# The token scale of two output norms: a block turn, two DRAM round trips and GpSimd in place of ones products, root and reciprocal

## The chip, the cores and the metric

The kernel runs on one core of a Trainium2 chip, as one launch. The metric is the device time of one execution in microseconds (us). The engines named below are TensorE (PE, matrix products), VectorE (DVE), ScalarE (ACT), GpSimd (POOL) and SyncE (SP, which only issues transfers). Each engine works through its own instruction list in order; an instruction whose inputs are not there holds everything behind it on that engine. TensorE's list and, in parts of the program, those of the other engines are in the order in which the program was written; elsewhere a scheduler sets the order when the program is built.

## What is computed

One layer of a bidirectional encoder: a combined input projection, eight attention heads, a gated linear recurrence in both directions, an RMS norm of each of the two groups, gates, and an output projection. The lines that bear on this change:

```python
def rms_norm(x, w):
    y = x * lax.rsqrt(jnp.mean(x * x, axis=-1, keepdims=True) + EPS)
    return y * w

mixed = jnp.concatenate([rms_norm(attn_out, attn_norm_w) * jax.nn.silu(g_attn),
                         rms_norm(lru_out, lru_norm_w) * jax.nn.silu(g_lru)], axis=-1)
return x + jnp.einsum('bse,ed->bsd', mixed, w_out)
```

There are 512 tokens; each group is 1024 wide. In the kernel both groups lie with features on the 128 partitions and tokens along the row, so a token's mean of squares is a sum over partitions (and over eight feature tiles), and its 1/rms is wanted on every partition.

## The kernel before, in words

Almost all the time is products in three parts (each float32 factor is split into a high and a low half, `mm3`, lines 153 to 155). Weights come as raw tiles `wr` of 128x2x512 through SP (`wraw`, line 206) into a ring of three; ACT casts the high half `wh` (line 218), DVE subtracts for the low half `wl` (line 219), and TensorE multiplies. A raw slot is free again once DVE has subtracted from it.

The stages in order: the recurrence's input projections, k and v, q in two halves (`both`), then the gate projections (`gates`) into which the attention is woven, the last gate projection (`later` woven in), and the output products (line 1029).

The group scales are made twice. For the recurrence group, `kv` runs beside the q projections: `lru_squares` sums squares into `hsum` (DVE line 568, POOL line 570), and then `halved` (lines 821 and 822) splits that sum, `spread` lets TensorE multiply both halves by a matrix of ones (line 829), which leaves the token's sum on all partitions, ACT takes the root (line 830) and DVE the reciprocal in four pieces (line 834). The result is `gbc`, 128x512. `normed` (line 839) multiplies the recurrence outputs `hs` by it on DVE. For the attention group the same happens in `later`, with `asum` (POOL line 751) in, and `normed` on the attention outputs `av`.

Two other things stand beside this. Sums of quarters of the output weights are built in DRAM by transfers that add (`add_to`, line 905): POOL issues them, 128x512 each, and SP copies what they add to. And at the very start, `busy` (line 1156) lets TensorE multiply ones while the first data are on the way: 11 such fillers (`WARM`) and then 3 (`WARM2`) between the first four turning products (line 253) and the first real products (line 388).

The order around the change: TensorE's is written out by hand. SP's, POOL's, ACT's and DVE's are the scheduler's near the first place (about 205 to 260 us), and SP's is by hand in the attention and POOL's, ACT's and DVE's by the scheduler near the second (about 420 to 460 us).

Of the kernel before, what the change touches and what calls it, by code (L numbers as in the profile page):

```python
# [11 lines left out]
F32 = mybir.dt.float32  # L12
F32R = mybir.dt.float32r
AF = mybir.ActivationFunctionType
ALU = mybir.AluOpType
AX = mybir.AxisListType

P = 128
SEQ = 512
DM = 2048  # L20
KT = DM // P
NT = SEQ // P
HD = 128
NH = 8
NKV = 2
G = NH // NKV
NB = 8
EPS = 1e-6
# [11 lines left out]
SOON = 150  # L40


WARM, WARM2 = 11, 3


BEGIN, STEPS, LATE = 11, 2, 3
# [5 lines left out]
B = 32  # L52
TURNED = 5
NQ = P // B
# [9 lines left out]
def hybrid_kernel(  # L64
# [20 lines left out]
    nc = tc.nc  # L85
# [4 lines left out]
    pools, order = {}, {"left": [], "right": []}  # L90

    def opened(name, side):
        pools[name] = tc.alloc_tile_pool(name=name, bufs=1, side=side, reuse_waits="tile")
        order[side].append(name)
        return pools[name]
# [18 lines left out]
    dram = ctx.enter_context(tc.tile_pool(name="dram", bufs=1, space=bass.MemoryType.DRAM))  # L114
# [3 lines left out]
    def nm(s):  # L118
        cnt[0] += 1
        return f"{s}_{cnt[0]}"  # L120
# [22 lines left out]
    def mm():  # L143
        return ps.tile([P, SEQ], F32, tag="mm", name=nm("mm"))

    def const(shape, name, dt=F32):
        return cp.tile(list(shape), dt, tag=name, name=name)

    def f(ap):
        return ap.bitcast(F32)  # L150
# [11 lines left out]
    ones_r = const([P, P], "ones_r", F32R)  # L162
    nc.gpsimd.memset(f(ones_r), 1.0)
    nhalf = const([P, 48], "nhalf")
# [44 lines left out]
    turn_of, split_done = [0], {}  # L209
# [33 lines left out]
    def behind(those):  # L243
        stack = ExitStack()
        for ins in those:
            stack.enter_context(tc.issue_after(ins))
        return stack
# [44 lines left out]
    def bring_back(to, aside_):  # L292

        src = aside_.rearrange("(i c) b x -> b c i x", c=B)
        for b in range(NQ):
            nc.sync.dma_start(
                to[b * B : (b + 1) * B].rearrange("p i k t r -> p i (k t r)"), src[b]
            )

    def in_order(v):  # L300
        return v.rearrange("p (t i r) -> p i t r", t=NT, i=NQ)
# [40 lines left out]
    last_pool = [None]  # L342
# [86 lines left out]
    def drain(fill):  # L429
        for _ in fill:  # L430
            pass
# [30 lines left out]
    sums = {}  # L462
# [97 lines left out]
    def lru_squares():  # L560

        hsum = pools["rot"].tile([P, 2, SEQ], F32, tag="hsum", name="hsum")
        nc.scalar.activation(hsum, hp[0], AF.Square)
        for pair in hp[1:]:
            yield 2
            sq = pools["rot"].tile([P, 2, SEQ], F32, tag="hsq", bufs=1, name=nm("hsq"))
            nc.scalar.activation(sq, pair, AF.Square)
            nc.vector.tensor_add(hsum, hsum, sq)
        sums["l"] = hsum[:, 0, :]
        nc.gpsimd.tensor_add(sums["l"], sums["l"], hsum[:, 1, :])  # L570
# [29 lines left out]
    def norm_rope(es, nh, tab):  # L600

        es = [e[:, : nh * HD].rearrange("p (h d) -> p h d", d=HD) for e in es]
        rs = []
        for e in es:
            r = pools["rot"].tile([P, nh], F32, tag=f"rr{nh}", bufs=NT, name=nm("rr"))
            for h in range(nh):
                sq = pools["rot"].tile([P, HD], F32, tag="sh", bufs=1, name=nm("sh"))
                nc.scalar.activation(sq, e[:, h, :], AF.Square, accum_out=r[:, h : h + 1])
            rsqrt_mean(r, r, HD, nh)
            rs.append(r)  # L610
        for t, (e, r) in enumerate(zip(es, rs)):
            sq = pools["rot"].tile([P, nh, HD], F32, tag="sq", bufs=2, name=nm("sq"))
            nc.vector.tensor_mul(e, e, r[:, :, None].broadcast_to([P, nh, HD]))
            for s in range(2):
                nc.vector.tensor_mul(
                    sq.rearrange("p h (a s d) -> p h a s d", s=2, d=32)[:, :, :, s, :],
                    e.rearrange("p h (a s d) -> p h a s d", s=2, d=32)[:, :, :, 1 - s, :],
                    tab[:, t, 1, :].rearrange("p (a s d) -> p a s d", s=2, d=32)[:, None, :, s, :]
                    .broadcast_to([P, nh, 2, 32]),
                )  # L620
            nc.vector.tensor_mul(e, e, tab[:, t, 0, :][:, None, :].broadcast_to([P, nh, HD]))
            nc.vector.tensor_add(e, e, sq)
        return es

    kth, ktl = [None] * NKV, [None] * NKV
# [5 lines left out]
    def sent(es, nh, *us):  # L631

        us = us or [
            pools["rot"].tile([P, NQ, 2, NT, B], F32, tag="uq", bufs=2, name=nm("uq"))
            for _ in range(nh // 2)
        ]
        for n, u in enumerate(us):
            for t, e in enumerate(es):
                blocks(u, t, e[:, 2 * n : 2 * n + 2].rearrange("p h d -> p (h d)"))
            yield  # L640
            asides.append(put_aside(u, "qd", 5))

    def landed(aside_):

        to = pools["qkv"].tile([P, NQ, 2, NT, B], F32, tag="lq", bufs=2, name=nm("lq"))
        bring_back(to, aside_)
        return to

    def split_head(pair, k, hi, lo):
        src = pair[:, :, k]  # L650
        hi, lo = (in_order(v) for v in (hi, lo))
        return nc.scalar.copy(hi, src).ins, nc.vector.tensor_sub(lo, src, f(hi)).ins

    def kv(es):
        turned_k = sent(norm_rope(es, NKV, rk), NKV)
        yield 20
        opened("wx", "right")
        for t in range(NT):
            vv = es[t][:, NKV * HD :]
            vt = pools["qkv"].tile([P, 2, NKV * HD], F32R, tag="v", bufs=NT, name=nm("v"))  # L660
            vh[t], vl[t] = vt[:, 0, :], vt[:, 1, :]
            nc.scalar.copy(vh[t], vv)
            nc.vector.tensor_sub(vl[t], vv, f(vh[t]))
        yield from lru_squares()
        yield 2
        drain(turned_k)
        yield 6
        pair = landed(asides.pop(0))
        for h in range(NKV):
            yield (12, 4)[h]  # L670
            kt = pools["qkv"].tile([P, 2, SEQ], F32R, tag="kt", bufs=NKV, name=nm("kt"))
            kth[h], ktl[h] = kt[:, 0, :], kt[:, 1, :]
            those = split_head(pair, h, kth[h], ktl[h])
        parts = halved(
            sums["l"],
            lambda: pools["rope"].tile([P, SEQ], F32R, tag="kv", bufs=NT, name=nm("kv")),
            those,
        )
        yield 4
        spread(gbc, parts, NB * P)  # L680

    qs = {}

# [127 lines left out]
    def fin_s(shape=(P, SEQ), dt=F32):  # L811
        return pools["fin"].tile(list(shape), dt, tag="s", bufs=2, name=nm("s"))

    eps = const([P, 48], "eps")
    nc.gpsimd.memset(eps, EPS)

    def halved(src, tile_of, those=()):

        hi, lo = tile_of(), tile_of()
        with behind(those):  # L820
            nc.scalar.copy(hi, src)
            nc.vector.tensor_sub(lo, src, f(hi))
        return hi, lo

    def spread(dst, parts, n, those=()):

        pb = mm()
        for k, part in enumerate(parts):
            nc.tensor.matmul(pb, ones_r, part, start=k == 0, stop=k == 1)  # L829
        nc.scalar.activation(dst, pb, AF.Sqrt, scale=1.0 / n, bias=eps[:, :1])  # L830
        for t in range(NT):
            ts_ = slice(t * P, (t + 1) * P)
            with behind(those):
                nc.vector.reciprocal(dst[:, ts_], dst[:, ts_])

    gbc = const([P, SEQ], "gbc")

    def normed(pair):
        nc.vector.tensor_mul(pair, pair, gbc[:, None, :].broadcast_to([P, 2, SEQ]))
# [372 lines left out]
    for step in proj_feat(C_XR, a1, first, given):  # L1212
# [8 lines left out]
        c, e = step  # L1221
# [123 lines left out]
    def build(i, pair, parts):  # L1345
        mixed[i][1] = parts
        seven(pair, *parts)
# [5 lines left out]

    def later():
        with tc.high_priority():
            parts = halved(sums["a"], lambda: fin_s(dt=F32R))
        yield 2
        with tc.high_priority():
            spread(gbc, parts, NH * HD, split_done[turn_of[0] - 2][1:])
        yield 4  # L1360
        for pair in ap_[:2]:
            normed(pair)
        yield 4
        todo = gate(late, ap_[:2], R_AN, fin_s)
        for _ in range(3):
            yield next(todo)
        build(4, ap_[0], [hring.tile([P, 7, H], F32R, name=nm(t)) for t in ("mh", "ml")])
        yield from todo
        for pair in ap_[2:]:
            normed(pair)  # L1370

    acc = []
    wsums = last_sums()
    fill = with_sums(proj_feat(C_GA + SEQ, acc, take=take), 1, 8, 8 + 2 * NP)
    weave(fill, later())
    drain(fill)
    closed("xw")
# [71 lines left out]
```

## Time and profile before

| | us |
|---|---|
| median of three runs (626.97, 627.20, 628.66) | 627.2 |
| the profiled execution | 626.85 |
| its span, first to last instruction | 625.1 |
| DVE busy | 494.5 |
| ACT busy | 352.5 |
| POOL busy | 101.7 |

The profile shows one execution. The span is the time between the first and the last instruction; the 1.75 us between span and execution lie outside it. In a row of the timeline the first number is the start, the second how long the row lasts (the first start to the last end, where several instructions are merged, with their count after an x), then engine, line, operation, what is written and read, and in brackets how long the engine sat idle before and what released it. A matrix product of 512 columns is recorded with some 0.39 us, but starts follow each other every 0.23 us, since they are pipelined.

### The profile page before, as it was taken

What the parts mean: (1) busy time and instruction counts of PE and PEld (TensorE: products, weight loads), DVE (VectorE), ACT (ScalarE), POOL (GpSimd) and SP (SyncE); (2) the same over time, 40 slices, a digit from 0 to 9 for tenths busy, and PEclk for the clock granted to TensorE, in tenths of its full rate; (3) what the DMA queues carried; (4) which work ended last, traced back from release to release, by engine and by line L of the source; (5) the groups of instructions that cost most, each with busy time, mean ns of one, the idle gap of its engine ahead of it and who ended that gap; (6) DMA issues with size and microseconds to landing.
All of it is one profiled execution on the core that took longest, in us unless ns stands there. A gap on an engine that the chain in (4) does not pass through costs nothing.

```text
span 625.1 us, 8277 instructions
## 1 busy us (share of the span) xinstructions
PE 619.9 (99%) x2756; PEld 512.5 (82%) x2756; DVE 494.5 (79%) x796; ACT 352.5 (56%) x617; POOL 101.7 (16%) x134
## 2 busy tenths in 40 slices
PE   9999999999999999999999999999999999999997
PEld 7888888888888888888888888888888888888886
DVE  5967979986699875987887888549978866886886
ACT  3764899379935823555475447428445633443441
POOL 0000211112003622622122222100310101010010
PEclk9999999999999999999999999999999999999999
DMA  8987775859774599489668646923995676896262
GB/s 289 303 227 224 182 198 171 179 134 198 233 232 139 169 245 242 104 204 271 187 179 254 201 143 192 265 76 107 270 243 183 209 253 228 297 339 226 70 202 101
DMA packets 73595, 127.61 MB, mean 204 GB/s; under 512 B 6617, under 2 KB 29265, under 8 KB 73553
## 3 DMA queue, kind: packets, MB, share of 16 engines
q1 hardware_dynamic: 65664, 109.65, 56.8%
q0 software_dynamic: 7712, 17.31, 14.3%
q8 instruction: 21, 0.34, 0.2%
q14 instruction: 22, 0.17, 0.1%
q10 hardware_dynamic: 176, 0.14, 0.1%
HBM read 110.29 MB, written 37.75 MB: 237 GB/s over the span
## 4 chain that ended last, share of the span: by engine, by line
PE 99%; ACT 0%; DVE 0%; issue 0%; POOL 0%; POOLq 0%
PE pj L153 20%; PE pj L155 20%; PE pj L154 20%; PE mm L1029 14%; PE pj L1029 11%; PE mm L155 3%; PE mm L153 3%; PE mm L154 3%; PE pj L388 2%; PE mm L253 1%; PE mm L1156 0%; PE mm L829 0%; ACT x L258 0%; PE mm L367 0%; DVE cb L1058 0%
## 5 line engine op out<-in xcount | busy, mean ns | idle before, releaser
L153 PE MATMUL pj<-x,wh 128*128 128x512 f32 x368 | 143.5, 390 | 0.0
L155 PE MATMUL pj<-x,wl 128*128 128x512 f32 x368 | 143.2, 389 | 0.0
L154 PE MATMUL pj<-x,wh 128*128 128x512 f32 x368 | 143.2, 389 | 0.0
L218 ACT CAST wh<-wr 128x512 fp32r<-128x512 f32 x142 | 84.5, 617 | 79.3 <-PE pj L154 31.7
L219 DVE TENSOR_TENSOR wl<-wr,wh 128x512 fp32r<-128x512 f32 x144 | 99.5, 720 | 19.6 <-ACT wh L218 18.5
L881 ACT CAST wh<-wr 128x1024 fp32r<-128x1024 f32 (+1 forms) x72 | 60.7, 861 | 75.0 <-PE mm L1029 37.5
L882 DVE TENSOR_TENSOR wl<-wr,wh 128x1024 fp32r<-128x1024 f32 (+1 forms) x72 | 68.7, 984 | 30.3 <-ACT wh L881 30.0
L155 PEld LDWEIGHTS pj<-x,wl 128*128 128x128 f32 x368 | 69.1, 188 | 14.5
L154 PEld LDWEIGHTS pj<-x,wh 128*128 128x128 f32 x368 | 69.1, 188 | 14.3
L153 PEld LDWEIGHTS pj<-x,wh 128*128 128x128 f32 x368 | 69.1, 188 | 14.2
L153 PE MATMUL pj<-wh,x 128*128 128x512 f32 x192 | 74.7, 389 | 0.0
L155 PE MATMUL pj<-wh,x 128*128 128x512 f32 x192 | 74.7, 389 | 0.0
L154 PE MATMUL pj<-wl,x 128*128 128x512 f32 x192 | 74.7, 389 | 0.0
L905 POOL DMA_DIRECT2D t<-in_w_out_dram x40 | 33.6, 906 | 157.7 <-DMA t<-in_w_out_dram 99.9
L1029 PE MATMUL mm<-wh,ml 128*128 128x512 f32 x126 | 49.0, 389 | 0.0
L1029 PE MATMUL mm<-wh,mh 128*128 128x512 f32 x126 | 49.0, 389 | 0.0
L1029 PE MATMUL mm<-wl,mh 128*128 128x512 f32 x126 | 49.0, 389 | 0.0
L154 PEld LDWEIGHTS pj<-wl,x 128*128 128x128 f32 x192 | 36.0, 188 | 7.6
L155 PEld LDWEIGHTS pj<-wh,x 128*128 128x128 f32 x192 | 36.0, 188 | 7.5
L153 PEld LDWEIGHTS pj<-wh,x 128*128 128x128 f32 x192 | 36.0, 188 | 7.4
L706 POOL TENSOR_SCALAR p<-p,sm 128x512 f32<-128x512 f32 x32 | 24.3, 762 | 89.3 <-DVE sm L705 89.3
L1029 PE MATMUL pj<-wl,mh 128*128 128x512 f32 (+1 forms) x100 | 38.5, 385 | 0.0
(201 smaller groups left out, 1050.8 us busy)
## 6 DMA issues: line engine op xcount, KB each, us to landing
wr<-in_w_in_dram SPq DMA_DIRECT2D x71, 512.0 KB, 5.0
wr<-in_w_out_dram SPq DMA_DIRECT2D x24, 512.0 KB, 5.2
t<-in_w_out_dram POOLq DMA_DIRECT2D x40, 256.0 KB, 7.3
wr<-t SPq DMA_DIRECT2D x40, 256.0 KB, 5.6
pd<-u SPq DMA_DIRECT2D x16, 512.0 KB, 3.0
pt<-pd SPq DMA_DIRECT2D x64, 128.0 KB, 3.9
t<-in_w_out_dram SPq DMA_DIRECT2D x24, 256.0 KB, 5.3
t<-t SPq DMA_DIRECT2D x16, 256.0 KB, 5.4
```

What stands on the lines that cost most here:

```text
L153: nc.tensor.matmul(acc, lh, rh, start=start, stop=False)
L154: nc.tensor.matmul(acc, lh, rl, start=False, stop=False)
L155: nc.tensor.matmul(acc, ll, rh, start=False, stop=stop)
L218: copy(hi, raw[:, k, :]).ins,
L219: nc.vector.tensor_sub(lo, raw[:, k, :], f(hi)).ins,
L253: nc.tensor.transpose(pt[:, t * P : (t + 1) * P], xc[:, t, ks], ident)
L388: nc.tensor.matmul(acc[e], w[:, e * P : (e + 1) * P], x_[2 * c + k], start=c == k == j == 0, stop=False,)
L706: last_pool[0] = nc.gpsimd.tensor_scalar(p, p, sm, 0.0, op0=ALU.mult, op1=ALU.add).ins
L881: nc.scalar.copy(hi[:, to], b)
L882: nc.vector.tensor_sub(lo[:, to], b, f(hi[:, to]))
L905: nc.gpsimd.dma_start(dst, src, accum_op=ALU.add)
L1029: nc.tensor.matmul(dst[s][:, es], lh[:, ts_], rh[:, es], start=i == ends_[0] and j == 0, stop=i == ends_[1] and j == 2,)
```

## The change

`halved` and `spread` are replaced by `token_scale`. It turns the 128x512 sums in blocks of 32x32 on DVE, so that in each quarter of the partitions a row is one token of a block, and sums each block's 32 columns (128x16). These four partial sums per token go to DRAM and come back side by side on 32 partitions (first round trip). GpSimd adds the four, scales, adds EPS and raises to the power -0.5 on a 32x16 tile. The 512 results go to DRAM as one row and come back to all 128 partitions (second round trip), and GpSimd copies them into `gbc` in token order. It is a generator: its parts are set between other steps by `next`. The fillers before the first products go from 3 to 5.

```diff
-WARM, WARM2 = 11, 3
+WARM, WARM2 = 11, 5
...
+        scale = token_scale(
+            gbc, sums["l"], NB * P,
+            lambda: pools["rope"].tile([P, SEQ], F32, tag="kv", bufs=NT, name=nm("kv")),
+        )
         for h in range(NKV):
-            yield (12, 4)[h]
+            for n in ((3, 3, 3, 3), (2, 2))[h]:
+                yield n
+                if (h, n) != (1, 2):
+                    next(scale)
...
-            those = split_head(pair, h, kth[h], ktl[h])
-        parts = halved(sums["l"], ..., those)
-        yield 4
-        spread(gbc, parts, NB * P)
+            split_head(pair, h, kth[h], ktl[h])
...
+    def token_scale(dst, src, n, tile_of):
+        turned, small = tile_of(), tile_of()
+        nj = SEQ // B
+        nc.vector.transpose(turned, src)
+        part = small[:, :nj]
+        nc.vector.reduce_sum(part, turned.rearrange("p (j c) -> p j c", c=B), axis=AX.X)
+        there = dram.tile([NQ, B, nj], F32, name=nm("parts"), tag="parts")
+        row = dram.tile([1, SEQ], F32, name=nm("row"), tag="row")
+        nc.sync.dma_start(there.rearrange("b r j -> (b r) j"), part)
+        yield
+        back = small[:B, 2 * B : 2 * B + NQ * nj].rearrange("r (b j) -> r b j", b=NQ)
+        nc.sync.dma_start(back, there.rearrange("b r j -> r b j"))
+        s = small[:B, 5 * B : 5 * B + nj]
+        with tc.issue_after(last_pool[0]):
+            nc.gpsimd.tensor_add(s, back[:, 0], back[:, 1])
+        for b in range(2, NQ):
+            nc.gpsimd.tensor_add(s, s, back[:, b])
+        nc.gpsimd.tensor_scalar(s, s, 1.0 / n, EPS, op0=ALU.mult, op1=ALU.add)
+        nc.gpsimd.tensor_tensor(s, s, nhalf[:B, :nj], op=ALU.pow)
+        yield
+        nc.sync.dma_start(row.rearrange("o (r j) -> (o r) j", j=nj), s)
+        yield
+        nc.sync.dma_start(turned, row.broadcast_to([P, SEQ]))
+        nc.gpsimd.tensor_copy(
+            dst.rearrange("p (j r) -> p j r", r=B), turned.rearrange("p (r j) -> p j r", j=nj)
+        )
+        yield
...
-            parts = halved(sums["a"], lambda: fin_s(dt=F32R))
-        yield 2
-        with tc.high_priority():
-            spread(gbc, parts, NH * HD, split_done[turn_of[0] - 2][1:])
-        yield 4
+            scale = token_scale(gbc, sums["a"], NH * HD, fin_s)
+            next(scale)
+        for _ in scale:
+            yield 3
```

TensorE's list loses two products at line 829 in each of the two places and gains two fillers; otherwise it is the same. On the other engines the scheduler places the new steps.

On POOL, beside the second half of the q projection, before: eleven adding transfers in a row (`t`), then the rms of the next q heads (`rr`).

```order
L347 TENSOR_TENSOR rr_2139<-rr_2139,nhalf 128x4
L905 DMA t_105<-in_w_out_dram 128x512 x8
L905 DMA t_106<-in_w_out_dram 128x512 x3
L346 TENSOR_SCALAR rr_2506<-rr_2506 128x4
L347 TENSOR_TENSOR rr_2506<-rr_2506,nhalf 128x4
```

The same place in the change (`kv_2252` is the small tile of `token_scale`, `kv_2251` the turned one):

```order
L917 DMA t_105<-in_w_out_dram 128x512 x6
L834 TENSOR_TENSOR kv_2252<-kv_2252 32x16
L917 DMA t_105<-in_w_out_dram 128x512
L836 TENSOR_TENSOR kv_2252<-kv_2252 32x16
L917 DMA t_105<-in_w_out_dram 128x512
L836 TENSOR_TENSOR kv_2252<-kv_2252 32x16
L917 DMA t_106<-in_w_out_dram 128x512
L837 TENSOR_SCALAR kv_2252<-kv_2252 32x16
L917 DMA t_106<-in_w_out_dram 128x512
L838 TENSOR_TENSOR kv_2252<-kv_2252,nhalf 32x16
L917 DMA t_106<-in_w_out_dram 128x512
L843 COPY gbc<-kv_2251 128x512
```

The five small steps and the copy stand among the adding transfers, one after each from the sixth on: the power stands behind the tenth, the copy behind the eleventh.

On DVE at the same stage, before: `wl_2591` and `wl_2595` are the low halves of the two weight tiles with which the first gate projection begins.

```order
L219 TENSOR_TENSOR wl_2469<-wr_2462,wh_2468 128x512
L219 TENSOR_TENSOR wl_2591<-wr_2588,wh_2590 128x512
L834 RECIPROCAL gbc<-gbc 128x128 x4
L219 TENSOR_TENSOR wl_2595<-wr_2588,wh_2594 128x512
L839 TENSOR_TENSOR hs_884<-hs_884,gbc 128x1024
L839 TENSOR_TENSOR hs_1083<-hs_1083,gbc 128x1024
L839 TENSOR_TENSOR hs_1443<-hs_1443,gbc 128x1024
L219 TENSOR_TENSOR wl_2601<-wr_2598,wh_2600 128x512
```

In the change the same two low halves are called `wl_2597` and `wl_2601`:

```order
L219 TENSOR_TENSOR wl_2475<-wr_2468,wh_2474 128x512
L851 TENSOR_TENSOR hs_886<-hs_886,gbc 128x1024
L851 TENSOR_TENSOR hs_1085<-hs_1085,gbc 128x1024
L851 TENSOR_TENSOR hs_1445<-hs_1445,gbc 128x1024
L219 TENSOR_TENSOR wl_2597<-wr_2594,wh_2596 128x512
L851 TENSOR_TENSOR hs_1698<-hs_1698,gbc 128x1024
L219 TENSOR_TENSOR wl_2601<-wr_2594,wh_2600 128x512
L219 TENSOR_TENSOR wl_2607<-wr_2604,wh_2606 128x512
```

The reciprocal is gone; both low halves now stand behind products with `gbc`, the first behind three of them, the second behind four.

On SP at that stage in the change (`lq` are transfers that bring turned q heads back):

```order
L289 DMA qd_2188<-uq_2177 128x1024
L840 DMA row_2256<-kv_2252 32x16
L206 DMA wr_2604<-in_w_in_dram 128x2x512
L296 DMA lq_2624<-qd_2182 32x4x256
L842 DMA kv_2251<-row_2256 128x512
L296 DMA lq_2624<-qd_2182 32x4x256
L206 DMA wr_2614<-in_w_in_dram 128x2x512
```

Before, the transfer of the weight tile (`wr`) and the eight `lq` followed the two `qd` directly; now the row goes out ahead of them, and its return stands behind one weight tile and one `lq`.

More of the change, by code (lines that the diff above doesn't have):

```diff
@@ L668, in kv @@
         pair = landed(asides.pop(0))
+        scale = token_scale(
+            gbc,
+            sums["l"],
+            NB * P,
+            lambda: pools["rope"].tile([P, SEQ], F32, tag="kv", bufs=NT, name=nm("kv")),
+        )
         for h in range(NKV):
[L670 removed]
+            for n in ((3, 3, 3, 3), (2, 2))[h]:
+                yield n
+                if (h, n) != (1, 2):
+                    next(scale)
             kt = pools["qkv"].tile([P, 2, SEQ], F32R, tag="kt", bufs=NKV, name=nm("kt"))
             kth[h], ktl[h] = kt[:, 0, :], kt[:, 1, :]
[L673 to L680 removed]
+            split_head(pair, h, kth[h], ktl[h])
     qs = {}
@@ L815, in hybrid_kernel @@
     nc.gpsimd.memset(eps, EPS)
[L817 to L834, printed above, removed]
+    def token_scale(dst, src, n, tile_of):
[25 more added lines that the diff above has]
+        yield
     gbc = const([P, SEQ], "gbc")
```

## The prediction

> **What bounds the kernel now.** I read the page's busy times first, then the chain that ended last, then who waited for whom on TensorE.
>
> ```profile
> span 625.1 us, 8277 instructions
> ...
> PE 619.9 (99%) x2756; PEld 512.5 (82%) x2756; DVE 494.5 (79%) x796; ACT 352.5 (56%) x617; POOL 101.7 (16%) x134
> ...
> PE 99%; ACT 0%; DVE 0%; issue 0%; POOL 0%; POOLq 0%
> ...
> PE mm L1156 <- POOL ones L161: 1.1, 1, 1.1
> ```
>
> TensorE is busy for 619.9 of 625.1 us and makes up 99% of the chain; the only wait of its own that the profile lists is the first 1.1 us. So two rules for the sum: a product taken out of TensorE's list saves its whole pitch, and anything that keeps TensorE waiting, anywhere, is added whole, since no idle time later on can absorb it.
>
> **What TensorE loses and gains.** The products by ones, from the timeline and the line's own view:
>
> ```profile
> 236.31 0.62 PE L829 MATMUL mm<-kv,ones_r 128*128 128x512 f32 x2
> 236.77 0.40 PE L153 MATMUL pj<-wh,x 128*128 128x512 f32 x1
> ...
> L829 PE MATMUL mm<-s,ones_r x2: 392/392/393, 427.3 to 427.6; 128*128 128x512 f32 x2
> ```
>
> The pair takes 236.77 - 236.31 = 0.46 us of TensorE. The pair at 427.3 is of the same form and length. Twice 0.46 is **-0.92 us**, certain as far as the list goes.
>
> The fillers:
>
> ```profile
> 1.13 2.53 PE L1156 MATMUL mm<-ones 128*128 128x256 bf16 x11 [1.13 <-POOL ones L161]
> 4.71 0.85 PE L1156 MATMUL mm<-ones 128*128 128x256 bf16 x3
> 4.96 0.69 ACT L258 ACTIVATE x<-mm,nw 128x512 fp32r<-128x512 f32 x1 [2.25 <-PE mm L253]
> 5.70 1.23 PE L388 MATMUL pj<-x,wh 128*128 128x512 f32 x4
> ```
>
> Eleven fillers last 2.53 us, at most 0.23 each. Three from 4.71 on have been streamed by about 5.4; the first real product starts at 5.70, just after ACT ends its input at 4.96 + 0.69 = 5.65. Two more fillers need 0.46 and find about 0.3 of idle time: they end near 5.86. I take **+0.1 us**; the ends are 0 (the first product's weights load under the fillers) and +0.46 (it is pushed back by all of both). What hides them is ACT's 0.69; without it they would cost 0.46.
>
> **The chain that makes the scale, first place.** This is where the time is decided. Its head is early. POOL finishes `hsum` at 205.05 + 1.63 = 206.7; a turn of 128x512 lasts 0.71 and a sum over such a row no more than the 0.68 of other DVE rows of that size, so the partial sums are ready near 209. Out and back through DRAM ahead of or between the weight loads there, they are on POOL before 225. The tail hangs on POOL's list, in which the power now stands behind the tenth adding transfer:
>
> ```profile
> 217.35 2.62 POOL L905 DMA_DIRECT2D t<-in_w_out_dram  x3
> 224.38 0.82 POOL L905 DMA_DIRECT2D t<-in_w_out_dram  x1 [4.41 <-issue]
> ...
> 227.79 0.81 POOL L905 DMA_DIRECT2D t<-in_w_out_dram  x1 [1.32 <-issue]
> 233.10 0.83 POOL L905 DMA_DIRECT2D t<-in_w_out_dram  x1 [4.51 <-issue]
> 234.43 0.82 POOL L905 DMA_DIRECT2D t<-in_w_out_dram  x1 [0.49 <-issue]
> 236.83 0.81 POOL L905 DMA_DIRECT2D t<-in_w_out_dram  x1 [1.59 <-issue]
> 242.03 0.82 POOL L905 DMA_DIRECT2D t<-in_w_out_dram  x1 [4.39 <-issue]
> 244.00 0.84 POOL L905 DMA_DIRECT2D t<-in_w_out_dram  x1 [1.15 <-issue]
> ...
> DMA to landing us min/median/max: 6.7/8.5/9.3
> ```
>
> The last line is the view of these eleven alone. They go out by threes: the fourth starts 7.0 us after the first, the seventh 8.7 after the fourth, the tenth 8.9 after the seventh, each time about one landing. So I read: three may be under way, and POOL stands still until the third last has landed. The small steps wait with them. Before, nothing on POOL was in a hurry; now the scale is.
>
> The tenth was issued at 242.03. In the change SP is silent from about 226 (it stands at the row, which waits for the power), so the eight `lq` and two weight loads that ran beside these transfers are not there, and a landing should be nearer the 6.7 than the 8.9: I take 6.5 after 233.1, so 239.6, plus 0.8 of issue: the power starts at **240.4** (between 238, if the seventh gains too, and 242.9, as before).
>
> The power itself on a 32x16 tile has no row. The nearest:
>
> ```profile
> 196.11 0.69 POOL L347 TENSOR_TENSOR rr<-rr,nhalf 128x2 f32<-128x2 f32 x1
> 207.78 1.02 POOL L347 TENSOR_TENSOR rr<-rr,nhalf 128x4 f32<-128x4 f32 x1
> ```
>
> Two columns 0.69, four 1.02: if that slope of 0.16 holds per column, sixteen cost 0.69 + 14 x 0.16 = 2.9; if it is mostly start-up, about 1. I take 2.5, nearer the slope, since two row lengths are all there is. Then the row to DRAM and the broadcast back, and the copy. Sizes near them:
>
> ```profile
> out_dram<-cb SPq DMA_DIRECT2D x1, 128.0 KB, 2.3
> vec_st<-in_conv_w_dram SPq DMA_DIRECT2D x1, 16.0 KB, 4.4
> out_dram<-xt SPq DMA_DIRECT2D x2, 256.0 KB, 2.6
> wr<-t SPq DMA_DIRECT2D x40, 256.0 KB, 5.6
> ...
> L706 POOL TENSOR_SCALAR p<-p,sm x32: 695/698/1577, 269.8 to 391.8; 128x512 f32<-128x512 f32 x32
> ```
>
> The row: 2.3 to 4.4, I take 2.4 (SP and POOL have little else under way just then). The broadcast writes 256 KB of SBUF and is issued about 2 us behind a weight tile of 512 KB: 2.6 to 5.6, I take 4.2. The copy: 0.7 by the row with one input, up to 1.6 with the strided read; 0.9. With 0.3 for three handovers `gbc` is ready at 240.4 + 2.5 + 2.4 + 4.2 + 0.9 + 0.3 = **250.7**; the ends, all costs at one side together, are 244.6 (238 + 1 + 2.3 + 2.6 + 0.7) and 257.4 (242.9 + 2.9 + 4.4 + 5.6 + 1.6).
>
> [...]
>
> [...]
>
> **Who waits for it.** DVE works in order, and the low halves with which the first gate projection begins now stand behind three and four products with `gbc`.
>
> ```profile
> 233.77 0.69 DVE L219 TENSOR_TENSOR wl<-wr,wh 128x512 fp32r<-128x512 f32 x1 [3.71 <-ACT wh L218]
> 237.69 3.39 DVE L834 RECIPROCAL gbc<-gbc 128x128 f32<-128x128 f32 x4 [3.23 <-ACT gbc L830]
> 241.00 0.63 DVE L219 TENSOR_TENSOR wl<-wr,wh 128x512 fp32r<-128x512 f32 x1
> 241.54 3.48 DVE L839 TENSOR_TENSOR hs<-hs,gbc 128x1024 f32<-128x1024 f32 x3
> ...
> 245.74 1.22 DVE L839 TENSOR_TENSOR hs<-hs,gbc 128x1024 f32<-128x1024 f32 x1
> ...
> 250.85 0.39 PE L155 MATMUL pj<-x,wl 128*128 128x512 f32 x1
> ...
> 251.53 0.39 PE L155 MATMUL pj<-x,wl 128*128 128x512 f32 x1
> ```
>
> TensorE takes up these tiles at 250.85 and 251.53 (line 155 with `wl` as weights). Before, DVE had them done at 234.5 and 241.6: 16 and 10 us ahead. In the change DVE starts on `gbc` when it comes, needs 3.4 for three products, 0.6 for the first low half, 1.2 for the fourth product and 0.6 for the second low half: done 5.8 after `gbc`. TensorE, earlier by 0.46 - 0.1, wants it at 251.2. So the scale has to be there by 251.2 - 5.8 = **245.4**, and each us later is a us of the kernel. With 250.7 the wait is **+5.3 us**. What queues behind DVE and ACT at that point (the next low halves, the second q half's rotation, the evacuation of the q products) is wanted at 256 and later and moves with TensorE's own delay; I add nothing. The freed 3.4 us of reciprocal, ACT's root and cast, and 0.7 of DVE for the split were beside TensorE: worth nothing by themselves.
>
> **The second place.** The sum of squares is ready when POOL ends it, and no adding transfer stands in front:
>
> ```profile
> 419.77 1.29 POOL L751 TENSOR_TENSOR asum<-asum,p 128x512 f32<-128x512 f32 x1 [15.27 <-ACT p L750]
> 421.54 0.68 DVE L471 TENSOR_TENSOR ev<-pj,rbc 128x512 f32<-128x512 f32 x1
> ...
> 442.69 1.28 DVE L219 TENSOR_TENSOR wl<-wr,wh 128x512 fp32r<-128x512 f32 x2
> ...
> 444.23 1.22 DVE L839 TENSOR_TENSOR av<-av,gbc 128x1024 f32<-128x1024 f32 x1
> ...
> 447.31 0.39 PE L155 MATMUL pj<-x,wl 128*128 128x512 f32 x1
> ```
>
> Turn and sum end near 423.6 (one evacuation stands between), out and back 2 x 2.4, five steps on POOL 1 + 2.5, row 2.4, broadcast 4.2, copy 0.9: 439.4, at worst 444. DVE reached the product with `gbc` at 444.2 before and, 2 to 3 us lighter, reaches it near 441 now. The low halves behind two of these products end 3.6 later and are wanted at 446.9, so `gbc` may come as late as about 443. The weight loads that SP now issues behind the row are for three tiles ahead. I take 0; at worst +1.
>
> **Sum.** 625.1 - 0.92 + 0.1 + 5.3 = 629.6 for the span. The profiled execution lasted 1.75 more than its span (626.85), so 631.3; the median shown, 627.2, is 0.35 above that execution, and half of that goes on top: **631.5 us**.
>
> **Rivals.**
>
> *The scale comes in time.* If the ring empties faster once SP is silent and the power costs about 1, `gbc` is there at 244.6 to 245.4 and DVE still meets TensorE. Then only -0.92 + 0.1 is left: 626.0 to 626.5. For it: the silence of SP is real, and 16 and 10 us of lead stood there. Against it: the tenth transfer at 242.03 leaves 3.4 us for power, two transfers and copy, and even at 238 only 7.4. It decides at 245.4. Chance 0.25.
>
> *Both places hold.* Should transfers be as slow at 430 as the weight tiles were at 232 (8.3 us and more), the second scale comes near 446, and 3 us follow on the first wait: 634.5. Against it: few transfers run there. Chance 0.07.
>
> *The products by ones were hidden, or the fillers cost all of theirs.* Then with no wait the time stays at 626.9 to 627.2. Against it: the pitch at 236.77 and the 99%. Chance 0.03.
>
> **How the numbers follow.** The forecast case, a wait at the first place between 2 and 9.5 us, has the remaining 0.65, and by itself lies between 628.2 and 636 (a wait of 9.5; later than that, all costs would have to fall on one side). Within 0.3% (1.9 us, about what a measurement of this kernel can tell from no change) are the first and the third rival and the lower edge of the forecast, about 0.05 of it. Slower by over 0.3%: 0.60 + 0.07 = 0.67. Faster by over 0.3% would need 1.9 us where the removed products hold 0.92: 0.04, for what I have not seen. Same: 0.29. The range reaches from the rival in time to the upper end of the wait: 626.1 to 636.0.
>
> **What would show it.** Right: one wait on TensorE at line 155 near 251 us, for DVE `wl`, of about 5 us; DVE idle from about 230 to 250 before the first `hs` product, released by POOL's copy; the power's row starting behind the tenth `t` transfer near 240; SP's row at about 243 and weight tiles behind it late by 10 us and more. The chain of waits would then leave TensorE once, through DVE, POOL and SP. Wrong: a TensorE without waits and a span near 624.3 (the copy came before 245.4), or a wait at another line. The power's own row settles 1 against 2.9, and the landings of row and broadcast settle the two transfer terms.

## The result, and the profile after

The changed kernel takes 638.11 us (median of 5, 637.0 to 638.36) against 628.56 for the kernel before (5 runs beside them, 626.97 to 629.06): 1.016 times, interval 1.0147 to 1.0174. Predicted were 631.5, range 626.1 to 636.0. The sign and the first cause were right, the size was not: the span grew by 11.2 us where 4.5 were forecast. Executions of the kernel before lie between 626.7 and 629.1 us, and the profiled one, 626.85, is among the shortest, so the spans lie further apart than the medians.

The page of the changed kernel (span, granted clock in 40 slices, chain by engine):

```profile
span 636.3 us, 8296 instructions
...
PEclk9999999999999999799999999999999999999999
...
PE 54%; DMA 3%; issue 3%; POOL 3%; DVE 3%; ACT 2%; SPq 0%; ACTq 0%; POOLq 0%; DVEq 0%
```

Before, 99% of the chain was TensorE. Now the chain leaves it, and one slice (the 17th, 254 to 270 us) has a clock of 7 tenths. The view of waits on TensorE (total, times, longest):

```profile
PE pj L155 <- DVE wl L219: 5.2, 2, 4.6
...
PE pj L153 <- ACT wh L218: 1.0, 1, 1.0
PE pj L153 <- ACT ev L596: 0.7, 1, 0.7
```

The first line is the wait that was predicted (4.65 of it is the first of the two); the other two lines were not. On TensorE's timeline at those places:

```profile
251.34 0.50 PE L153 MATMUL pj<-x,wh 128*128 128x512 f32 x1 [0.66 <-ACT ev L596]
...
256.73 0.79 PE L155 MATMUL pj<-x,wl 128*128 128x512 f32 x1 [4.65 <-DVE wl L219]
257.32 0.63 PE L153 MATMUL pj<-x,wh 128*128 128x512 f32 x1
257.75 0.63 PE L154 MATMUL pj<-x,wh 128*128 128x512 f32 x1
...
451.10 0.50 PE L153 MATMUL pj<-x,wh 128*128 128x512 f32 x1 [0.99 <-ACT wh L218]
...
458.32 0.50 PE L155 MATMUL pj<-x,wl 128*128 128x512 f32 x1 [0.53 <-DVE wl L219]
```

The product that started at 250.85 before starts at 256.73, and the two behind it are 0.43 apart instead of 0.23. The one that started at 447.31 starts at 458.32, 11.0 later. Set start by start against the trace of before, the 11.2 us of span come in these steps: +0.6 in the first 45 us, -0.46 for each of the two pairs of products by ones, +0.8 at 251.34, +4.9 and +0.5 for two low halves, +2.7 while products are 0.43 apart, and +2.6 between 440 and 460 (two waits of 1.0 and 0.5, and products beside them 0.34 apart).

The chain of the first scale on POOL's timeline, the power and the copy:

```profile
239.00 3.23 POOL L838 TENSOR_TENSOR kv<-kv,nhalf 32x16 f32<-32x16 f32 x1
...
251.49 1.05 POOL L843 COPY gbc<-kv 128x512 f32<-128x512 f32 x1 [8.17 <-DMA kv<-row]
```

Between the two, on SP's queue, the row and the broadcast:

```profile
242.26 0.33 SPq L840 DMA_DIRECT2D row<-kv  x1
...
244.91 0.33 SPq L842 DMA_DIRECT2D kv<-row  x1
```

DVE's timeline behind it:

```profile
252.58 3.50 DVE L851 TENSOR_TENSOR hs<-hs,gbc 128x1024 f32<-128x1024 f32 x3 [22.26 <-POOL gbc L843]
255.99 0.68 DVE L219 TENSOR_TENSOR wl<-wr,wh 128x512 fp32r<-128x512 f32 x1
256.59 1.22 DVE L851 TENSOR_TENSOR hs<-hs,gbc 128x1024 f32<-128x1024 f32 x1
257.73 1.28 DVE L219 TENSOR_TENSOR wl<-wr,wh 128x512 fp32r<-128x512 f32 x2
258.93 0.68 DVE L613 TENSOR_TENSOR ev<-ev,rr 128x512 f32<-128x512 f32 x1
...
265.71 1.29 DVE L219 TENSOR_TENSOR wl<-wr,wh 128x512 fp32r<-128x512 f32 x2
...
272.72 1.29 DVE L652 TENSOR_TENSOR q<-lq,q 128x512 fp32r<-128x512 f32 x2
```

The rows at 258.93 (the rotation of the second q half) and 272.72 (the attention's first `q`) stood so in the kernel before:

```profile
250.87 0.69 DVE L613 TENSOR_TENSOR ev<-ev,rr 128x512 f32<-128x512 f32 x1 [3.91 <-POOL rr L347]
...
265.06 1.29 DVE L652 TENSOR_TENSOR q<-lq,q 128x512 fp32r<-128x512 f32 x2
```

DVE stands 22 us for `gbc`, and from 252.58 to the end of `q` at 274.0 it has no gap. The rotation begins 8.1 later than before, where DVE had 3.9 of slack ahead of it, and `q` comes 7.7 later.

ACT's timeline, where the evacuation of the q products (line 596) stands behind the cast of a weight tile that SP issued behind the row:

```profile
250.09 0.62 ACT L218 CAST wh<-wr 128x512 fp32r<-128x512 f32 x1 [9.61 <-DMA wr<-in_w_in_dram]
250.61 0.68 ACT L596 ACTIVATE ev<-pj,rstd 128x512 f32<-128x512 f32 x1
```

In the kernel before:

```profile
246.51 0.69 ACT L596 ACTIVATE ev<-pj,rstd 128x512 f32<-128x512 f32 x1 [1.42 <-PE pj L155]
```

The evacuation is 4.1 later, and TensorE waits for it at 251.34.

### The profile page after: what moved, and what is told of

It reads as the page before. It is cut to its first block, busy times and chain, and to the rows that moved or that the text cites. A ratio compares the mean times of both kernels' runs of the same rounds, so it can differ in the third digit from the quotient of the medians.

```text
span 636.3 us, 8296 instructions
## 1 busy us (share of the span) xinstructions
PE 624.3 (98%) x2754; PEld 513.7 (81%) x2754; DVE 488.2 (77%) x790; ACT 348.2 (55%) x611; POOL 115.4 (18%) x146
## 4 chain that ended last, share of the span: by engine, by line
PE 54%; DMA 3%; issue 3%; POOL 3%; DVE 3%; ACT 2%; SPq 0%; ACTq 0%; POOLq 0%; DVEq 0%
PE mm L1041 13%; PE pj L1041 10%; PE pj L155 8%; PE pj L153 8%; PE pj L154 8%; PE mm L153 2%; PE mm L155 2%; PE mm L154 2%; DMA wr<-in_w_in_dram 1%; DVE wl L219 1%; ACT wh L218 1%; DMA kv<-parts 1%; DMA s<-row 1%; ACT sh L608 1%; DVE hs L851 1%
## 5 line engine op out<-in xcount | busy, mean ns | idle before, releaser
L155 PE MATMUL pj<-x,wl 128*128 128x512 f32 x368 | 145.0, 394 | 5.3 <-DVE wl L219 5.2
L1041 PE MATMUL pj<-wh,mh 128*128 128x512 f32 (+1 forms) x100 | 38.5, 385 | 0.0
```

The source lines that it names most:

```text
L155: nc.tensor.matmul(acc, ll, rh, start=False, stop=stop)
L1041: nc.tensor.matmul(dst[s][:, es], lh[:, ts_], rh[:, es], start=i == ends_[0] and j == 0, stop=i == ends_[1] and j == 2,)
```

## The experiments

Twelve kernels ran. The edits are shown shortened. Ratios are against the kernel before on the same chip; "span" is that of the profiled execution.

**One place at a time, and the fillers alone.** First place as before:

```diff
-        scale = token_scale(gbc, sums["l"], ...)
+        parts = halved(sums["l"], ...); yield 4; spread(gbc, parts, NB * P)
```

> The first place has the split, ones products, root and reciprocal back; the second place and the fillers stay changed. Theory (three losses: 8.9 us at the first place, of which 5.7 are waits and 3.2 a TensorE at half clock after them; 2.6 at the second; 0.4 to 0.6 at the fillers): TensorE has no wait near 251 us and no stretch with 427 ns between products there; span 636.3 - 8.9 + 0.46 = 627.9, with the waits near 441 us still there. Rival (the first place only shifts a wait which DRAM traffic causes anyway, or the slow stretch at 256 has nothing to do with the wait): span above 630 with a slow stretch still in it.

Second place as before (the same edit in `later`):

> The second place has the split, ones products, root and reciprocal back; the first place and the fillers stay changed. Theory: the waits on ACT and DVE at TensorE near 450 us are the second place's own, 2.6 us; span 636.3 - 2.6 + 0.46 = 634.2. Rival (they are an after-effect of the first place's delay, for example of weight loads that stay late): the waits stay and the span stays above 636.

The kernel before with `WARM2 = 5`:

> The kernel before with five fillers in place of three at the second spot. Theory: the two fillers cost 0.2 to 0.5 us of TensorE in all (0.42 in the profiled run of the change): span 625.3 to 625.6, time not told apart from before. Rival (they hide under ACT, or bring the full clock sooner): span 625.1 or less.

Measured, in this order: 1.0036 (1.0025 to 1.0047), span 628.0, with the two waits of the second place (1.0 and 0.5) and none near 251; 1.0117 (1.0097 to 1.0138), span 633.1, with the wait near 251, the slow products, and none after 440; 0.9993 (0.9982 to 1.0005), span 625.7. The second span is 1.1 under its expectation: the wait for the evacuation near 251 was not there, and TensorE stood 0.2 for its first real input (`PE pj L388 <- ACT x L258: 0.2`), a wait that the changed kernel does not have, so its fillers were done sooner; by the 1.71 and 1.24 below I estimate some 0.5 for that. So the two places lose separately, about 8 and 2.6 us, and the fillers nothing that can be told.

The fillers' 0.6 of span needs another reading. The first four real products in four kernels, the first without extra fillers (row of before in the prediction: 1.23), the others with two more. On TensorE's timeline of the changed kernel:

```profile
5.70 1.71 PE L388 MATMUL pj<-x,wh 128*128 128x512 f32 x4
```

Of the kernel with the products later (below):

```profile
5.69 1.24 PE L388 MATMUL pj<-x,wh 128*128 128x512 f32 x4
```

Of the kernel with own tiles (below):

```profile
5.69 1.99 PE L388 MATMUL pj<-x,wh 128*128 128x512 f32 x4
```

All start at 5.69 or 5.70: the fillers push nothing. With the same list these four products last 1.24 to 1.99. In the changed kernel they start at 5.70, 6.29, 6.72 and 7.01, so 0.59, 0.43 and 0.29 apart, and later ones 0.23 (7.91, 8.14); in the kernel before the second starts at 6.06 and the third 0.23 behind it. The time from which products are 0.23 apart, here called the opening of the clock, differs from one profiled execution to the next.

**The second place.** ACT's timeline there in the changed kernel:

```profile
449.91 0.63 ACT L807 ACTIVATE s<-ev 128x512 f32<-128x512 f32 x1 [3.15 <-POOL gbc L843]
450.44 1.13 ACT L218 CAST wh<-wr 128x512 fp32r<-128x512 f32 x2
```

The gate's Silu (line 807) writes a tile of `fin_s`, of which there are two; the new `token_scale` has taken both and gives the last one back with its copy. ACT, in order, stands at the Silu, and behind it are the high halves that TensorE waits for at 451.10. The edit gives the scale tiles of its own:

```diff
-            scale = token_scale(gbc, sums["a"], NH * HD, fin_s)
+            own_ = iter(["wh0", "wl0"])
+            scale = token_scale(gbc, sums["a"], NH * HD, lambda: <tile of "fin" under next(own_)>)
```

> The changed kernel, but the two tiles of the second token scale are tiles of their own (not the pair that the attention gate's Silu writes afterwards). Theory (the second place lost its 2.6 us because ACT stood at the Silu, whose output tile the scale still held, with the casts of two weight tiles behind it): no wait of TensorE between 440 and 460 us, ACT's casts there near 444 to 447, span 636.3 - 2.6 = 633.7; the first place is as in the changed kernel (about 5 us at line 155 near 251). Rival (the late scale itself holds DVE there, through the av products): the waits of 2.6 us stay, span 636.3.

Measured: 1.012 (1.0095 to 1.0145), span 634.5. ACT's list then, its casts 5 us earlier even than the 444 to 447 expected:

```profile
437.27 0.62 ACT L807 ACTIVATE s<-ev 128x512 f32<-128x512 f32 x1
439.20 1.32 ACT L218 CAST wh<-wr 128x512 fp32r<-128x512 f32 x2 [1.31 <-issue]
```

No wait between 430 and 460 is left; the second place is worth the -0.5 of its two products. The span is 0.8 over the expectation because the first products were slow (1.99 above) and the first wait was 5.5. With the first place as before and the same tiles:

> The first place as before, the second as changed but with tiles of its own: what the second place is worth when its scale holds nobody up. Theory: no wait of TensorE between 430 and 460 us, only the pair of products by ones gone there; span 628.0 (the run with the first place undone) - 2.6 = 625.4, between 624.7 and 626 by where the clock opens at the start. Rival (the second scale is late for the av products by itself): a wait of 1 us or more between 440 and 460, span 626.5 or more.

Span 625.0, 0.9996 (0.9986 to 1.0005): no wait there, and `gbc` ready at 441.8 is early enough for the `av` products.

**POOL's order at the first place.** The additions, the power and the copy go ahead of the adding transfers:

```diff
-        with tc.issue_after(last_pool[0]):
-            nc.gpsimd.tensor_add(s, back[:, 0], back[:, 1])
+        with tc.high_priority():
+            with tc.issue_after(last_pool[0]):
+                nc.gpsimd.tensor_add(s, back[:, 0], back[:, 1])
...
+            last_pool[0] = nc.gpsimd.tensor_tensor(s, s, nhalf[:B, :nj], op=ALU.pow).ins
```

> The changed kernel, but POOL's steps of the scale (four additions and steps, the power, the copy) go ahead of the adding transfers that stand in front of them. Theory (the scale is late because POOL's steps stand behind a ring of adding transfers): power between 225 and 231 us, copy done near 241, no wait at line 155 near 251, no stretch at half clock, span 636.3 - 5.4 - 3.5 = 627.4 with the second place's 2.6 left in. Rival (the two round trips by themselves take too long beside the weight loads): the copy ends after 247, a wait of 2 us or more stays at line 155 near 251, span 630 or more.

Measured: 1.0073 (1.0052 to 1.0095), span 629.6. POOL's timeline:

```profile
225.50 2.93 POOL L839 TENSOR_TENSOR kv<-kv,nhalf 32x16 f32<-32x16 f32 x1
...
241.97 1.06 POOL L845 COPY gbc<-kv 128x512 f32<-128x512 f32 x1 [11.83 <-DMA kv<-row]
...
251.41 0.84 POOL L919 DMA_DIRECT2D t<-in_w_out_dram  x1 [0.83 <-DVE wl L219]
252.32 0.19 POOL L346 TENSOR_SCALAR rr<-rr 128x4 f32<-128x4 f32 x1
```

The power came 13.5 earlier, `gbc` only 9.5: the broadcast, issued at 230.3 behind a weight tile and two `qd`, took 11.6 to the copy. The wait at 251 and the slow stretch are gone (granted clock 1.0 over the span, against 0.994 in the changed kernel), as the theory had it. A wait of 1.2 for `q` is new: the adding transfers, held up behind the copy, now stand in front of the q heads' `rr`, which begin at 252.32 (249.53 before). The span is 2.2 over its expectation: 1.4 at this wait, 0.6 in the first 45 us, 0.2 at low halves. With both edits:

> The changed kernel with both edits: POOL's steps ahead of the adding transfers, and tiles of their own for the second scale. Theory (both losses are separate, and without them only the removed products and the fillers are left): 627.4 - 2.6 = 624.8 of span, no wait on TensorE over 0.5 us beside the first. Rival (the edits interact: the gain of one is lost at the other place): span 626 or more.

1.0051 (1.0032 to 1.007), span 629.0: missed by 4. The second place was clean, but `gbc` came at 244.1, 1.1 later than in the run before, while TensorE was 0.9 earlier, so that a low half was 2.0 late at 247.1; the granted clock was 0.50 for one stretch behind it (247.96 to 251.37).

**DVE's order.** The `hs` products behind the low halves of the first gate tiles, the scale as late as ever:

```diff
-                    normed(hp[k // 4 - 4])
+                    with behind(split_done[-1][1:]):
+                        normed(hp[k // 4 - 4])
```

> The changed kernel, but the four products of hs with the scale stand behind the low halves of the first gate tiles on DVE; POOL, SP and the time of the scale stay. Theory (TensorE waits only because the low halves stand behind the products in DVE's order): the scale is as late as in the changed kernel (near 252), the wait at line 155 near 251 is gone and with it the stretch at half clock; a wait of about 0.8 for ACT's evacuation behind the late weight tile may stay; span 636.3 - 8.1 = 628.2. Rival (the late weight tiles behind the row on SP hold TensorE as well): a wait of 2 us or more between 250 and 260 stays, span 630 or more.

1.0139 (1.0118 to 1.0159), span 633.0, 4.8 over its expectation: the low-half wait and the slow stretch went (granted clock 1.0 over the span), but 4.5 us of others came or stayed. ACT's timeline:

```profile
249.74 0.62 ACT L218 CAST wh<-wr 128x512 fp32r<-128x512 f32 x1 [9.85 <-DMA wr<-in_w_in_dram]
```

The waits on TensorE in the same run:

```profile
PE mm L155 <- DVE q L652: 2.2, 1, 2.2
PE mm L154 <- DVE pl L728: 1.4, 1, 1.4
...
PE pj L153 <- ACT ev L596: 0.9, 1, 0.9
```

ACT stands 9.85 for the weight tile that SP issues only behind the row; the evacuations of q and their squares (`sh`) are behind that cast, so `rr`, the rotation and `q` are 3.7 late. This is the rival of that run, in part right. The `pl` wait is put down to the moved products, one of which (318.39) now stands ahead of that `pl` (321.13) on DVE; no run separates it.

**TensorE kept busy.** Are the slow products the clock? Fillers of 128x256 stand in front of the first gate product, 44 and then 58:

```diff
+    held = mm()
+    for _ in range(44):
+        nc.tensor.matmul(held[:, : 2 * P], wv[:, :P], wv, start=True, stop=True)
```

> The change with 44 more fillers of 128x256 on TensorE between the last q product and the first gate product, where TensorE waits; at 0.109 us each they last 4.8 us, less than the wait of 5.7. Theory (an idle TensorE of about 5 us is put to half clock at 256 us and gets the full clock back 6.8 us later): with the idle time filled the stretch with 427 ns between products is gone, the waits end where they did, and the span is about 3.2 us shorter, near 633. Rival (the slow stretch comes from memory traffic or from the weights, not from idleness): the stretch stays and the span is 636 or more.

> The changed kernel with 58 fillers of 128x256 ahead of the first gate product (44 in the run before), so that no window of 3.41 us there is less than half busy. Theory of the clock (a window in which TensorE is about half idle or more is followed by one at half clock): fillers end near 256.5, the waits for low halves add up to less than in the run with 44, the clock stays at 1.00 throughout, products 227 ns apart from about 258.7 on, span 637.0 - 1.7 = 635.3. Rival (the slow products there have another cause, weight loads or transfers beside them): products 427 ns apart after 258.5 again, a stretch at half clock stays, span near 637.

Measured: 1.0182 (1.016 to 1.0204), span 637.0, and 1.0199 (1.0177 to 1.0222), span 636.8: 4 and 1.5 over the expectations. Windows at the clock's own edges in the changed kernel (from:to, length, TensorE busy and its rows, granted clock, share and GB/s of transfers):

```profile
249.18:252.59 3.41, 2.25 (x9) 1.00 1.10 259
252.59:256.00 3.41, 0.00 (x0) 1.00 0.88 170
256.00:259.42 3.42, 2.60 (x5) 0.50 0.04 13
259.42:262.83 3.41, 3.41 (x9) 0.50 0.54 154
```

With 44 fillers:

```profile
255.53:258.94 3.41, 1.73 (x7) 1.00 0.01 3
258.94:262.36 3.42, 3.42 (x10) 0.50 0.53 153
```

With 58 fillers:

```profile
267.51:270.93 3.42, 0.24 (x2) 1.00 0.96 120
270.93:274.34 3.41, 3.41 (x8) 0.50 1.01 217
```

In the changed kernel an idle window (0.00 of products) is followed by two at a granted clock of 0.50; with 44 fillers a half idle one (1.73) by one; with 58 the products are 0.23 apart from 256.4 to 267.3, with no slow one before 270.9. At 0.50 products are 0.43 apart. So in these runs the slow products are the clock's, behind TensorE's own idleness. The gain was lost again a little later. By the product at 267.33 TensorE was 3.3 ahead of the changed kernel; there it stands 3.2 for the next low half, and that idle window (0.24 of products) is followed by one at 0.50. TensorE's timeline of the run with 58:

```profile
270.90 0.79 PE L155 MATMUL pj<-x,wl 128*128 128x512 f32 x1 [3.18 <-DVE wl L219]
```

DVE's:

```profile
268.96 1.28 DVE L652 TENSOR_TENSOR q<-lq,q 128x512 fp32r<-128x512 f32 x2
270.17 2.49 DVE L219 TENSOR_TENSOR wl<-wr,wh 128x512 fp32r<-128x512 f32 x4
```

In the changed kernel DVE makes this low half at 265.71, ahead of the rest of the rotation and of `q`; here the scheduler has put it behind both. So these two runs show what slows the products, and not what the clock alone costs in the changed kernel.

**Row and broadcast together, then `rr` first.** On top of POOL's order and own tiles, SP issues the broadcast with one weight load behind the row:

```diff
-        nc.sync.dma_start(row..., s)
-        yield
-        nc.sync.dma_start(turned, row.broadcast_to([P, SEQ]))
+        with tc.high_priority():
+            nc.sync.dma_start(row..., s)
+            nc.sync.dma_start(turned, row.broadcast_to([P, SEQ]))
```

> The changed kernel with POOL's steps ahead of the adding transfers, tiles of their own for the second scale, and on SP the broadcast right behind the row with one weight load between them (in the run with POOL's steps first, a weight load and two more stood between, and the broadcast landed 11.6 us after its issue). Theory (both losses of the change are order and tiles, and a scale that arrives before 240 costs nothing): broadcast lands within 4 to 8 us, copy done between 234 and 238, no wait of TensorE over 0.5 us beside the first, no stretch at half clock, POOL's rr rows near 250 as before, span 625.1 - 0.92 = 624.2, up to 625.3 by where the clock opens at the start. Rival (SP's wait for the row, or the new order on DVE, opens another wait): a wait of 1 us or more somewhere between 240 and 270, span 626 or more.

1.0039 (1.0026 to 1.0051), span 627.7. The copy came at 235.18 and the `hs` products cost nothing; the rival's waits stood there, 0.7 and 1.8. POOL's timeline:

```profile
251.82 0.83 POOL L920 DMA_DIRECT2D t<-in_w_out_dram  x1 [3.72 <-issue]
252.73 0.19 POOL L346 TENSOR_SCALAR rr<-rr 128x4 f32<-128x4 f32 x1
```

POOL stood at its ring of adding transfers until 251.82, with `rr` behind it. One transfer moved:

```diff
-                yield
+                for _ in range(2 if to is t1 and m == 6 else 1):
+                    yield
```

> The run with row and broadcast together, and one adding transfer of POOL moved from ahead of the powers of the second q half (rr) to behind them. Theory (in that run the rr powers, and with them the rotation on DVE and the first q tile of the attention, were 3.2 us later than before because POOL stood at its ring of adding transfers): first rr power near 249.8 instead of 253.0, DVE's rotation from 250.9, the waits of 1.8 (q) and 0.7 (low half) gone, span 627.7 - 2.9 = 624.8, between 624.2 and 625.3 by where the clock opens. Rival (the rotation is late for another reason, or the moved transfer delays POOL's scaling of p at 270): a wait of 1 us or more stays between 255 and 275, span 626.5 or more.

POOL's timeline, and the only wait of TensorE that is left:

```profile
249.35 0.19 POOL L346 TENSOR_SCALAR rr<-rr 128x4 f32<-128x4 f32 x1 [1.14 <-ACT sh L608]
```

The view of waits:

```profile
PE mm L1172 <- POOL ones L161: 1.1, 1, 1.1
```

Span 624.7 (624.8 expected), 626.57 us against 627.17: 0.9985 (0.9977 to 0.9994). This version beats the changed kernel by about 11.5 us and the kernel before by some 0.15%, about what the four removed products are worth (0.92 us).

## Why the prediction was wrong, step by step

| step | predicted | measured |
|---|---|---|
| products by ones | -0.92 | -0.92 |
| fillers | +0.1 | 0 (+0.6 from where the clock opened) |
| power starts; lasts | 240.4; 2.5 | 239.0; 3.23 |
| row, to the broadcast's issue | 2.4 | 2.65 |
| broadcast, to the copy | 4.2 (2.6 to 5.6) | 6.6 |
| copy; `gbc` ready | 0.9; 250.7 | 1.05; 252.5 |
| wait for low halves | +5.3 | +4.9 and +0.5 |
| evacuation behind the late weight tile | nothing | +0.8 |
| products 0.43 apart | not seen | +2.7 |
| second place | 0, at worst +1 | +2.6 |
| span | 629.6 | 636.3 |

- **Right.** The pitch of the removed products; the power behind the tenth adding transfer, three of which are under way at a time by their starts (in the changed kernel the seventh 7.75 us after the fourth, the tenth 6.8 after the seventh, with landings of 6.0 to 9.2; start of the power 1.4 early, inside the ends given); DVE idle for about 20 us; one wait at line 155 near 251 of about 5; SP's row at 242.3; the shape of the chain at the first place. The rival "in time" fell. Its condition, `gbc` by 245.4, holds only for the order that was forecast: with POOL's steps first `gbc` was ready at 243.0 and that wait was gone, but with both edits 244.1 was too late, since the scheduler had put two of the `hs` products ahead of a low half that TensorE takes up at 245.2.
- **Terms mis-sized.** The broadcast left its range: 6.6 to the copy, and 11.6 with more transfers ahead of it. It stood beside weight loads and `lq`, and the prediction priced it by `wr<-t` over the whole run. The power lasted 3.23, above the slope's 2.9. `gbc` came 1.8 late by them. That the waits still add up to the forecast 5.3 is luck: TensorE, too, came to the second of the two products 2.0 later than forecast (0.5 from the start, 0.9 at the evacuation, 0.6 in slow products between the two). At the second place the row landed in 1.3; the broadcast landed in 6.5 at the first and 4.9 at the second.
- **The steps that failed are three terms that the sum put at nothing.** They make 6.1 of the 6.7 us between 629.6 and 636.3; the rest is mostly the clock's opening at the start. The measured 638.1 passes the upper end of the range by 2.1, less than either of the two large ones.
- **"Each us later is a us of the kernel" (+2.7).** The sum took a wait at its length alone. Here the window of 3.41 us without a product was followed by two at a granted clock of 0.50, in which products are 0.43 apart instead of 0.23. The profile of before has no idle window ahead of its end (TensorE busy for 619.9 of 625.1 us), so it could not warn of it.
- **"The second place: I take 0" (+2.6)** followed times, not tiles. The time held: `gbc` was ready at 449.9, which is 441.4 without the 8.5 that TensorE had lost by then (439.4 forecast, 443 allowed), and with own tiles nothing is lost. What cost 2.6 is that the scale's tiles come from `fin_s`, and so hold ACT's Silu and the casts behind it. The rival "both places hold" comes near with its 3 us, but its cause, a second scale that is late, was not there: its 8.3 us are of three weight tiles of 512 KB between 226 and 246 us in the kernel before (landed in 8.3 to 11.7), and the broadcast at the second place landed in 4.9.
- **"What queues behind DVE and ACT at that point ... moves with TensorE's own delay; I add nothing" (+0.8).** It did not move with TensorE: ACT stood 9.6 for a weight tile that SP had issued behind the row, and the evacuation of q was 4.1 late. The prediction itself said that such tiles would be 10 us late, and did not follow ACT's list behind their cast. On DVE, 22 us of standing end in a list without a gap, whose `q` is 7.7 late. In the changed kernel this costs nothing more, because TensorE is 9.1 late at its first product with `q`; with the products later, where DVE's list has gaps again, `q` is still 3.7 late by ACT's tile, and 2.2 of it is a wait.
- **Fillers:** the mechanism was wrong in both ends: nothing is pushed (5.69 or 5.70 with either number of fillers), and the four products behind them vary by 0.75 with the same list (1.24 to 1.99), more than the 0.46 that the fillers could cost.

Open: what the clock alone costs in the changed kernel. The runs with fillers changed the order of DVE's `q` and low halves too, so the 2.7 could not be split between clock and DVE's list. An estimate: TensorE is 9.1 late at its first product with `q` and DVE's `q` 7.7, so about 1.4 of the 2.7 would be saved, and the rest come back as a wait for `q`.

## What to carry to other kernels

When an engine is made to wait for a result that was early before, price the whole list behind that wait up to its next slack, on each engine that the wait or a silent queue holds, and not only the first consumer; and where TensorE idles, look for slow products behind the wait (here four windows of 3.41 us with 0, 0.24, 1.45 and 1.73 us of products were followed by a granted clock of 0.50). When scratch tiles are taken from a shared pool, ask who writes those buffers next and what stands behind that writer. Steps of a latency chain belong ahead of long transfers on each engine and queue they cross; here four such orders (POOL's power, SP's broadcast, POOL's `rr`, ACT's tiles) decided 11 us, and the work saved was worth 1.

## What the hardware showed that I had not expected

- The granted clock changes by windows. In the changed kernel its edges at 256.00, 262.83 and 634.88 us lie 6.83 and 372.05 apart, 2 and 109 times 3.413; the slow stretches with 44 fillers, with 58 and with both edits last 3.42, 3.41 and 3.41, and begin at 258.94, 270.93 and 247.96, so the phase differs between executions. A window at full clock with TensorE busy for 0, 0.24, 1.45 or 1.73 us was followed by one at 0.50; with 1.77 ("row and broadcast together", 265 us), 1.99 (products later, 320 us) or 2.25 (the changed kernel, 249 us) it was not. These are seven windows, in which the ends of products are modelled: too few for a threshold. At half clock the window busy for 2.60 of 3.42 was followed by another half one, and the four that were busy throughout by one at full clock. The two windows around the 2.0 us wait of the run with both edits:

```profile
244.54:247.96 3.42, 1.45 (x7) 1.00 0.57 80
247.96:251.37 3.41, 3.41 (x10) 0.50 1.04 162
```

  The 2.0 us wait of the run with both edits cost 1.6 more in slow products behind it (eight some 0.42 apart instead of 0.23), and the 2.2 us wait with the products later cost none (granted clock 1.0 over that span).
- The power -0.5 on 32x16 took 2.92 to 3.52 us on POOL, on 128x4 mostly 1.01 to 1.46 (up to 1.90) and on 128x2 0.69 to 0.96: over these three shapes it grew with the columns, though 32x16 has a quarter of the partitions.
- The row of 2 KB landed 1.3 us after its issue at the second place; at the first, in the changed kernel, the broadcast that waits for it is issued 2.65 behind it. The broadcast of 256 KB landed in 4.3 to 4.9 at the second place and in 6.3 to 6.5 at the first; with POOL's steps first 11.6 passed from its issue there (230.34) to the copy (241.97). The 11.6 had a weight tile and two stores of 512 KB issued between the row and it, and the 6.3 one weight tile alone.
